# Gate and up: a second set of weight sums, two more raw tiles, accumulators cleared in another order, residual rows kept in DRAM meanwhile

## The chip, the core and the metric

The kernel runs on one core of a Trainium2 chip. Its time is the device time of one execution, in microseconds (us). TensorE (PE) does the matmuls, VectorE (DVE) and ScalarE (ACT) work on tiles, GpSimd (POOL) and SyncE (SP) here mostly issue DMA transfers. Each engine takes its instructions in the order in which they were written to it, and waits where a semaphore is not yet set.

## The reference

One decoder layer over 256 tokens of width 2048, all in float32. The edit lies in the feed-forward part, the third of four:

```python
x = x + mixed @ w_o[i]                        # attention and S5, before it
hf = rms_norm(x, g_ffn_norm[i])
x = x + (jax.nn.silu(hf @ w_gate[i]) * (hf @ w_up[i])) @ w_down[i]   # D_FF = 5632
gate = jax.nn.sigmoid(rms_norm(x, g_ple_norm[i]) @ w_ple_gate[i])    # after it
x = x + gate * (p[i] @ w_ple_proj[i])
```

`x` before the feed-forward part is the residual; in the kernel it is `xs`, four tiles of 128x1024 (512 KB each), which are next needed when the first output block of `w_down` is done.

## The kernel before

**Splitting.** Products keep float32 accuracy by splitting each operand into a high and a low part: ScalarE writes `w_hi` (a rounding copy, L195), VectorE writes `w_lo = w_raw - w_hi` (L196), and each product is three matmuls (hi hi, lo hi, hi lo). The activations `hf` stand in SBUF as `fh` and `fl`.

**Chunks.** Weights come in chunks of 256 rows by 512 columns (512 KB, a tile of 128x2x512), listed in the order of use. `load_to` issues their DMAs on SP into `RAW` = 5 rotating buffers `w_raw`; `split_to` splits them into `PART` = 3 rotating pairs; `take(i)` hands chunk i to PE, after calling for splits and loads ahead of it.

**Gate and up.** 11 blocks of 512 columns. A block has 8 pairs j = 0 to 7, each a gate chunk and an up chunk of the same rows. It adds into four PSUM accumulators: `acc[0]` and `acc[2]` are the gate halves of the two groups of 128 tokens, `acc[1]` and `acc[3]` the up halves. A plain pair is 24 matmuls of 128x512. The pairs in `MIXED` (j = 2, 4, 6; in block 0 only 4, 6) use a Strassen-like scheme: `mix()` builds sums of the weight tiles (`w_sum` on VectorE, then split into `w_last` and two `w_mix`), and seven products replace eight; four more PSUM banks `pp_p` hold shared products, which `shared()` combines into `wsg` and `uc` when a block's last mixed pair is done.

**End of a block.** For each token group t: `wsg += acc[2t]` (VectorE), silu (ScalarE), `uc = acc[2t+1] - uc` (VectorE), `wsg *= uc` (VectorE). Then `gate_task` transposes `wsg` by eight 128x128 matmuls into `pp_g`, and ScalarE copies it to a tile `g`, kept until the down projection. The PSUM banks of the accumulators rotate: the next block writes its `acc[0]`, then from its fourth matmul on `acc[2]`, and from the 13th on `acc[1]` and `acc[3]`, into the banks in the order in which the code releases them.

**Order of the work.** The code is written in the order of the model; a scheduler then orders each engine's instructions by priority and by its own estimate of when inputs are ready. `tc.high_priority(n)` moves instructions ahead; splits and mixing have `W_AHEAD` = 70. `Slots` S is a list of 39 SBUF tiles that the program hands out and takes back (`wait_get`, `wait_n`, `S.put`).

Of the kernel before, what the change touches and what calls it, by code (L numbers as in the profile page):

```python
# [11 lines left out]
F32 = mybir.dt.float32  # L12
F32R = mybir.dt.float32r
I32 = mybir.dt.int32
AF = mybir.ActivationFunctionType
ALU = mybir.AluOpType
# [26 lines left out]
class Slots:  # L43
    def __init__(self, pool, tags):
        self.pool, self.free, self.own = pool, deque(tags), {}
# [36 lines left out]


W_AHEAD = 70

AHEAD = {'s5_params': -50, 'x_stats': 50, 'glu_out': -25, 'gate_task': -25, 'norm_task': -100, 'latent_norms': -50, 'z_task': -200, 'head_norms': -200}

# [54 lines left out]
class Weights:  # L142
# [4 lines left out]
    def __init__(self, tc, pool, sched):  # L147
        self.tc, nc = tc, tc.nc
        self.nc, self.pool, self.sched, self.chunks = nc, pool, sched, []
        self.raw, self.part, self.n_dma, self.n_split = {}, {}, 0, 0  # L150
        self.extra, self.native = {}, set()
        self.mixed, self.kept, self.sums = set(), {}, None

    def block(self, w, k0, nk, c0, n):
        ids = []
# [9 lines left out]
    def load_to(self, i):  # L165
        while self.n_dma <= min(i, len(self.chunks) - 1):
            w, k, c0, n = self.chunks[self.n_dma]
            t = self.pool.tile([128, 2, n], F32, tag="raw", bufs=self.RAW, name="w_raw")
            self.nc.sync.dma_start(
                out=t, in_=w[k * 128:(k + 2) * 128, c0:c0 + n].rearrange("(k p) n -> p k n", p=128)  # L170
            )
            self.raw[self.n_dma] = t
            self.n_dma += 1
            for out, in_ in self.extra.pop(self.n_dma, ()):
                self.nc.sync.dma_start(out=out, in_=in_)

    def split_to(self, i):
        while self.n_split <= min(i, len(self.chunks) - 1):
# [14 lines left out]
            lo = self.pool.tile([128, 2, n], F32R, tag="w_lo", bufs=self.PART, name="w_lo")  # L193
            with self.tc.high_priority(W_AHEAD):
                self.nc.scalar.activation(out=hi, in_=raw, func=AF.Copy)  # L195
# [7 lines left out]
    def mix(self, g, u):  # L203


        V, A, s = self.nc.vector, self.nc.scalar, self.sched
        last, raws, parts = self.sums

        def add(o, a, b):
            V.tensor_tensor(out=o, in0=a, in1=b, op=ALU.add)  # L210

        def part(h, l, r):
            A.activation(out=h, in_=r, func=AF.Copy)  # L213
            V.tensor_tensor(out=l, in0=r, in1=h.bitcast(F32), op=ALU.subtract)  # L214

        with self.tc.high_priority(W_AHEAD):
            add(raws[0][:, 0], g[:, 0], u[:, 0])
            add(raws[0][:, 1], u[:, 0], u[:, 1])
            part(last[:, 0], last[:, 1], u[:, 1])
            add(raws[1][:, 0], raws[0][:, 0], u[:, 1])  # L220
            add(raws[1][:, 1], raws[1][:, 0], g[:, 1])
            for r, (h, l) in zip(raws, parts):
                part(h, l, r)
        s.act += 5 * 512 * 0.83e-3 + 3 * 0.19
        s.dve = max(s.dve + 9 * 512 * 1.05e-3 + 0.42, s.act)
        (h0, l0), (h1, l1) = parts
        return ((last[:, 0], last[:, 1]), (h0[:, 0], l0[:, 0]), (h0[:, 1], l0[:, 1]),
                (h1[:, 0], l1[:, 0]), (h1[:, 1], l1[:, 1])), None, s.dve

    def take(self, i):  # L230
        self.split_to(i + self.PART - 1)
        self.load_to(i + self.PART - 1 + self.RAW)
        hi, lo, t = self.part.pop(i)
        self.sched.pe = max(self.sched.pe, t)
        return hi, lo
# [3 lines left out]
def hybrid_layer_kernel(  # L239
# [6 lines left out]
    nc = tc.nc  # L246
# [7 lines left out]
    dram = ctx.enter_context(tc.tile_pool(name="scratch", bufs=1, space=bass.MemoryType.DRAM))  # L254

    S = Slots(big, [f"s{i}" for i in range(39)])
    PP = Slots(psb, [f"pp{i}" for i in range(4)])
    sched = Sched(tc)
    W = Weights(tc, wts, sched)

    blk = {}
# [28 lines left out]
    def wait_get(shape, name, dtype=F32):  # L290
        n = 0
        while True:
            t = S.try_get(shape, name, dtype)
            if t is not None:
                return t
            sched.step()
            sched.pe += 1.0
            n += 1
            if n > 2000:
                raise RuntimeError(f"no slot for {name}: {S.held()}")  # L300

    def wait_n(n, shape, name, dtype=F32):
        return [wait_get(shape, name, dtype) for _ in range(n)]
# [13 lines left out]
    def stat(name, *dims):  # L317
        return con.tile([128, *dims], F32, name=name)
# [3 lines left out]
    r_a, r_s, r_f, r_p = (stat(n, 2) for n in ("r_a", "r_s", "r_f", "r_p"))  # L322
# [10 lines left out]
    def size(ap):  # L333
        n = 1
        for d in ap.shape[1:]:
            n *= d
        return n
# [4 lines left out]
    def tt(o, a, b, op=ALU.mult):  # L342
        V.tensor_tensor(out=o, in0=a, in1=b, op=op)  # L343
        sched.dve += size(o) * 1.05e-3 + 0.1
# [9 lines left out]
    def act(o, i, f, **k):  # L354
        A.activation(out=o, in_=i, func=f, **k)  # L355
        sched.act += size(o) * 0.83e-3 + 0.19 + 0.09 * sum(n in k for n in ("accum_out",))
# [53 lines left out]
    def accs2():  # L410
        return [psa.tile([128, 512], F32, tag="acc", bufs=4, name="acc") for _ in range(2)]

    def block(ids, lhs, need=None):
        accs = accs2()
        for i, cid in enumerate(ids):
            if need is not None:
                need(W.chunks[cid][1])
            chunk(cid, accs, lhs, i == 0, i == len(ids) - 1)
        return accs
# [23 lines left out]
    NWU = 30  # L443
    X0, B0, NE = 18, 8, 22
    GATE = "y0"


    def s5_params():
# [145 lines left out]
    def s5_tables(rho):  # L594

        while "params" not in sched.flags or rho and GATE not in sched.flags:
            yield None
# [65 lines left out]
    def rot_tables(rho):  # L663

        while "params" not in sched.flags or rho and GATE not in sched.flags:
            yield None
# [452 lines left out]
    def tiles4(hi, lo, k0=0):  # L1119
        def lhs(k, t):  # L1120
            k -= k0
            s = slice(128 * t, 128 * t + 128)
            return hi[k // 4][:, k % 4, s], lo[k // 4][:, k % 4, s]
        return lhs
# [102 lines left out]
    acc = block(blk["zq"], lhs_h, need_h)  # L1227
# [3 lines left out]
    acc = block(blk["zkv"], lhs_h)  # L1231
# [6 lines left out]
    acc = block(blk["u"][0], lhs_h)  # L1238
# [3 lines left out]
    acc = block(blk["u"][1], lhs_h)  # L1242
# [26 lines left out]
    xs = [wait_n(2, [128, 1024], "xs") for _ in range(2)]  # L1269
# [13 lines left out]
    for p, (lo, hi) in enumerate(blk["woa"]):  # L1283
        acc = accs2(), accs2()
# [48 lines left out]
    for b in range(2):  # L1333
        acc = accs2() + accs2()
        ids = blk["glu"][b]
        for i, cid in enumerate(ids):
            w, k, c0, n = W.chunks[cid]
# [21 lines left out]
    fh = wait_n(4, [128, 4, 256], "fh", F32R)  # L1359
    fl = wait_n(4, [128, 4, 256], "fl", F32R)  # L1360
    rows = {j: wait_get([128, 2, 512], "sum", F32R) for j in MIXED}
# [5 lines left out]
    for b in range(4):  # L1367
        acc = block(blk["wos"][b], lhs_s, need_s)
# [6 lines left out]
    lhs_f = tiles4(fh, fl)  # L1375
    wsg = wait_n(2, [128, 2, 512], "wsg")
    uc = wait_get([128, 2, 512], "uc")
    W.sums = (wait_get([128, 2, 512], "w_last", F32R), wait_n(2, [128, 2, 512], "w_sum"),
              [wait_n(2, [128, 2, 512], "w_mix", F32R) for _ in range(2)])
    gr, gh, gl = [], [], []  # L1380

    def gate_task(b):
# [74 lines left out]
    def mixed_block(ids, lhs, rows, a, b, need):  # L1457
        acc = accs2() + accs2()
        pq, left = None, sum(i[2] in W.mixed for i in ids)
        n = left  # L1460
        for i, (j, cg, cu) in enumerate(ids):
            need(j)
            m = cu in W.mixed
            if m and pq is None:
                pq = [wait_pp("p") for _ in range(4)]
            pair(j, cg, cu, acc, pq + [left == n, left == 1] if m else None, lhs, rows, i == 0, i == len(ids) - 1)
            left -= m
            if m and left == 0:
                shared(pq, a, b)
        return acc  # L1470
# [4 lines left out]
    for b in range(11):  # L1475
        ws = wsg[b % 2]
        acc = mixed_block(blk["gu"][b], lhs_f, rows, ws, uc, need_f)
        if b == 0:
            total_rstd(r_f, ss_f)
        for t in range(2):  # L1480
            tt(ws[:, t], ws[:, t], acc[2 * t], ALU.add)
            act(ws[:, t], ws[:, t], AF.Silu, scale=r_f[:, t:t + 1])
            tt(uc[:, t], acc[2 * t + 1], uc[:, t], ALU.subtract)
            tt(ws[:, t], ws[:, t], uc[:, t])
        sched.add(gate_task(b), 0)
    S.put(*fh, *fl, *rows.values(), uc, W.sums[0], *W.sums[1], *W.sums[2][0], *W.sums[2][1])
    lhs_g = tiles4(gh, gl)

    def need_g(k):
# [9 lines left out]
    for b in range(4):  # L1499
        ph.append(wait_get([128, 4, 256], "ph", F32R))  # L1500
        pl.append(wait_get([128, 4, 256], "pl", F32R))
        acc = block(blk["down"][b], lhs_g, need_g)
# [14 lines left out]
    for c in range(4):  # L1517
        acc = block(blk["pp"][c], lambda k, t: (prh[:, k, 128 * t:128 * t + 128],
                                                prl[:, k, 128 * t:128 * t + 128]))
# [9 lines left out]
    for b in range(4):  # L1529
        acc = block(blk["ple"][b], lhs_h2, need_p)  # L1530
        if b == 0:
            total_rstd(r_p, ss_p)
        n = 256 if b == 3 else 512
# [88 lines left out]
```

## Time and profile before

| | |
|---|---|
| time, median of 3 runs | 1145.84 us (1144.41 to 1147.18) |
| profiled execution | 1146.05 us, span 1144.1 us, granted clock 0.998 |
| PE busy | 1117.7 us, 98% of the span |
| VectorE / ScalarE / POOL busy | 861.4 / 648.3 / 19.0 us |
| gate/up stage | 317.77 to 796.63 us in the span, 478.86 us |
| DMA | 216.97 MB, mean 190 GB/s |

A matmul is shown with a modelled duration of 0.39 us, longer than the pace at which matmuls follow each other, so that PE time is best read from start to start. In a timeline a row is: start, duration, engine, line, operation, output<-inputs, shape; the bracket at its end is the idle time of the engine before it and what ended it. A waits row is: waiting instruction <- what it waited for, total us, times, longest. A windows row is: the stretch, its length, the busy time of PE, PE's weight loads, VectorE, ScalarE and POOL with the count of instructions, then granted clock, DMA share and GB/s. `SPq` is SP's DMA queue.

### The profile page before, as it was taken

The numbers are of one execution on the slowest core, as the hardware profiler recorded it, in microseconds if no ns is written. First come the engines' busy times: TensorE is split into PE (matmuls) and PEld (weight loads), VectorE is DVE, ScalarE is ACT, GpSimd is POOL, SyncE is SP. The second block draws the span as 40 slices with busy tenths as digits, with TensorE's granted clock in tenths as the row PEclk, the third lists the DMA queues.
The fourth block names the chain that finished last, engine by engine and source line by source line (L and its number), as shares of the span: only waits on it lengthen the run. The fifth ranks groups of instructions, "written<-read, shape, count | busy, mean of one in ns | idle before, by whom it ended". The sixth has DMA issues, their size and how long they took to land.

```text
span 1144.1 us, 15655 instructions
## 1 busy us (share of the span) xinstructions
PE 1117.7 (98%) x5842; PEld 923.7 (81%) x5842; DVE 861.4 (75%) x1233; ACT 648.3 (57%) x921; POOL 19.0 (2%) x40
## 2 busy tenths in 40 slices
PE   9998999999999999999999999999999999999998
PEld 6877877889887877877877877878888888888886
DVE  7988999658698898888898898899645454546554
ACT  7863994636665555655655655557534344436443
POOL 1000020000000000000000000000000000000000
PEclk9999999999999999999999999999999999999999
DMA  9996471355566656665665665665665655555662
GB/s 336 247 259 191 117 229 33 109 190 179 183 187 200 204 184 185 204 196 180 211 192 178 210 186 178 217 183 184 202 194 186 197 188 191 188 192 187 213 209 91
DMA packets 112188, 216.97 MB, mean 190 GB/s; under 512 B 8032, under 2 KB 12912, under 8 KB 112112
## 3 DMA queue, kind: packets, MB, share of 16 engines
q1 hardware_dynamic: 109808, 211.23, 58.9%
q0 software_dynamic: 2304, 4.74, 1.5%
q8 instruction: 46, 0.75, 0.3%
q14 instruction: 30, 0.25, 0.1%
HBM read 212.66 MB, written 3.28 MB: 189 GB/s over the span
## 4 chain that ended last, share of the span: by engine, by line
PE 78%; DVE 9%; DMA 5%; ACT 4%; issue 2%; POOL 0%; DVEq 0%; SPq 0%; ACTq 0%; POOLq 0%
PE acc L359 67%; PE pp_p L359 5%; DMA w_raw<-in_w_up_dram 4%; DVE w_lo L196 3%; ACT w_hi L195 2%; DMA e<-in_bE_dram 1%; PE pp_g L386 1%; PE pp_at L359 1%; DVE w L750 1%; PE pp_at L1003 1%; PE pp_n L386 1%; PE pp_v L731 1%; DVE w_sum L210 1%; ACT L355 1%; PE pp_y L785 1%
## 5 line engine op out<-in xcount | busy, mean ns | idle before, releaser
L196 DVE TENSOR_TENSOR w_lo<-w_raw,w_hi 128x1024 fp32r<-128x1024 f32 (+2 forms) x350 | 420.8, 1206 | 207.4 <-ACT w_hi L195 206.1
L195 ACT ACTIVATE w_hi<-w_raw 128x1024 fp32r<-128x1024 f32 (+2 forms) x350 | 366.1, 1047 | 350.7 <-PE acc L359 318.9
L359 PE MATMUL acc<-w_hi,fh 128*128 128x512 f32 x480 | 188.7, 396 | 5.9 <-DVE uc L343 5.8
L359 PE MATMUL acc<-w_lo,fh 128*128 128x512 f32 x480 | 188.1, 392 | 0.0
L359 PE MATMUL acc<-w_hi,fl 128*128 128x512 f32 x480 | 187.1, 390 | 0.0
L359 PE MATMUL acc<-w_hi,gh 128*128 128x512 f32 x352 | 137.3, 390 | 0.0
L359 PE MATMUL acc<-w_hi,gl 128*128 128x512 f32 x352 | 137.1, 389 | 0.0
L359 PE MATMUL acc<-w_lo,gh 128*128 128x512 f32 x352 | 137.0, 389 | 0.0
L359 PEld LDWEIGHTS acc<-w_hi,fh 128*128 128x128 f32 x480 | 90.1, 188 | 30.9 <-DVE uc L343 12.4
L359 PEld LDWEIGHTS acc<-w_hi,fl 128*128 128x128 f32 x480 | 90.1, 188 | 18.8
L359 PEld LDWEIGHTS acc<-w_lo,fh 128*128 128x128 f32 x480 | 90.2, 188 | 17.5 <-DVE w_lo L196 0.2
L213 ACT ACTIVATE w_mix<-w_sum 128x1024 fp32r<-128x1024 f32 x64 | 67.9, 1062 | 50.3 <-DVE w_sum L210 38.5
L359 PEld LDWEIGHTS acc<-w_hi,gl 128*128 128x128 f32 x352 | 66.1, 188 | 13.8
L359 PEld LDWEIGHTS acc<-w_lo,gh 128*128 128x128 f32 x352 | 66.1, 188 | 13.6
L359 PEld LDWEIGHTS acc<-w_hi,gh 128*128 128x128 f32 x352 | 66.1, 188 | 13.6 <-DVE uc L343 0.2
L214 DVE TENSOR_TENSOR w_mix<-w_sum,w_mix 128x1024 fp32r<-128x1024 f32 x64 | 76.3, 1218 | 0.6
L359 PE MATMUL pp_p<-w_mix,sum 128*128 128x512 f32 x288 | 70.5, 389 | 0.0
L359 PEld LDWEIGHTS pp_p<-w_mix,sum 128*128 128x128 f32 x288 | 54.1, 188 | 11.2
L210 DVE TENSOR_TENSOR w_sum<-w_raw 128x512 f32<-128x512 f32 x64 | 42.2, 687 | 27.7 <-DMA w_raw<-in_w_up_dram 26.5
L359 PE MATMUL acc<-w_hi,ph 128*128 128x512 f32 x128 | 49.8, 389 | 0.0
L359 PE MATMUL acc<-w_lo,ph 128*128 128x512 f32 x128 | 49.8, 389 | 0.0
L359 PE MATMUL acc<-w_hi,pl 128*128 128x512 f32 x128 | 49.8, 389 | 0.0
(308 smaller groups left out, 1713.0 us busy)
## 6 DMA issues: line engine op xcount, KB each, us to landing
w_raw<-in_w_gate_dram SPq DMA_DIRECT2D x88, 512.0 KB, 4.2
w_raw<-in_w_up_dram SPq DMA_DIRECT2D x88, 512.0 KB, 4.6
w_raw<-in_w_down_dram SPq DMA_DIRECT2D x88, 512.0 KB, 3.7
w_raw<-in_w_o_dram SPq DMA_DIRECT2D x32, 512.0 KB, 3.7
w_raw<-in_w_ple_gate_dram SPq DMA_DIRECT2D x32, 512.0 KB, 4.1
w_raw<-in_w_in_dram SPq DMA_DIRECT2D x24, 512.0 KB, 7.6
w_raw<-in_w_glu_dram SPq DMA_DIRECT2D x8, 512.0 KB, 4.4
w_raw<-in_w_uq_dram SPq DMA_DIRECT2D x8, 384.0 KB, 3.5
```

The source lines that it names most:

```text
L195: self.nc.scalar.activation(out=hi, in_=raw, func=AF.Copy)
L196: self.nc.vector.tensor_tensor(out=lo, in0=raw, in1=hi.bitcast(F32), op=ALU.subtract)
L210: V.tensor_tensor(out=o, in0=a, in1=b, op=ALU.add)
L213: A.activation(out=h, in_=r, func=AF.Copy)
L214: V.tensor_tensor(out=l, in0=r, in1=h.bitcast(F32), op=ALU.subtract)
L355: A.activation(out=o, in_=i, func=f, **k)
L359: T.matmul(out=o, lhsT=a, rhs=b, start=start, stop=stop)
L386: T.transpose(out=o, in_=i, identity=ident if idt is None else idt)
L731: T.matmul(out=pv[p, r * 256 + i4 * 64:r * 256 + i4 * 64 + 64], lhsT=ee[r][p, i * 64:i * 64 + 64], rhs=um[p, i, :], start=True, stop=True, ...
L750: V.tensor_tensor_scan(out=w, data0=dc, data1=w, initial=0.0, op0=ALU.mult, op1=ALU.add)
L785: T.matmul(out=o, lhsT=a[p, i, :], rhs=f[p, i, :], start=False, stop=(r == 1), tile_position=(64 * s, 64 * s))
L1003: T.matmul(out=o, lhsT=a, rhs=b_, start=False, stop=(i == 1), skip_group_check=True)
```

## The change

1. Two more raw tiles `w_more` (from the slots): in the gate/up stage the chunks whose number is 0 or 3 modulo 7 land there, and `take()` calls for loads two chunks further ahead.
2. Two sets of `w_last` and `w_mix` (`NSET` = 2) in turn; `w_sum` stays shared. `take()` now calls for splits so that three plain chunks, and a mixed one behind them, are ready.
3. The end of a block is written in another order (both gate halves, both up halves, both products) and at a high priority, `G_AHEAD` = 100.
4. To make room, the four `xs` tiles are written to DRAM (`x_keep`) and their slots given to the `g` tiles from block 3 on; behind the stage they are read back. Both go by POOL's DMA queue.

```diff
+G_AHEAD = 100
...
-            t = self.pool.tile([128, 2, n], F32, tag="raw", bufs=self.RAW, name="w_raw")
+            if self.more and self.n_dma % 7 in (0, 3) and self.n_dma < self.more_end:
+                self.more.rotate(1)
+                t = self.more[0]
+            else:
+                t = self.pool.tile([128, 2, n], F32, tag="raw", bufs=self.RAW, name="w_raw")
...
-        last, raws, parts = self.sums
+        last, raws, parts = self.sums[0]
+        self.sums.rotate(1)
...
     def take(self, i):
-        self.split_to(i + self.PART - 1)
-        self.load_to(i + self.PART - 1 + self.RAW)
+        n, j = 0, i
+        while n < self.PART and j < len(self.chunks):
+            n += j not in self.mixed
+            j += 1
+        if j in self.mixed:
+            j += 1
+        self.split_to(j - 1)
+        self.load_to(j - 1 + self.RAW + len(self.more))
...
+    NSET = 2
...
-    W.sums = (wait_get([128, 2, 512], "w_last", F32R), wait_n(2, [128, 2, 512], "w_sum"),
-              [wait_n(2, [128, 2, 512], "w_mix", F32R) for _ in range(2)])
+    w_sum = wait_n(2, [128, 2, 512], "w_sum")
+    for _ in range(NSET):
+        W.sums.append((wait_get([128, 2, 512], "w_last", F32R), w_sum,
+                       [wait_n(2, [128, 2, 512], "w_mix", F32R) for _ in range(2)]))
+    W.more_end = blk["down"][0][0]
+    W.more.extend(wait_n(2, [128, 2, 512], "w_more"))
...
-        for t in range(2):
-            tt(ws[:, t], ws[:, t], acc[2 * t], ALU.add)
-            act(ws[:, t], ws[:, t], AF.Silu, scale=r_f[:, t:t + 1])
-            tt(uc[:, t], acc[2 * t + 1], uc[:, t], ALU.subtract)
-            tt(ws[:, t], ws[:, t], uc[:, t])
+        with tc.high_priority(G_AHEAD):
+            for t in range(2):
+                tt(ws[:, t], ws[:, t], acc[2 * t], ALU.add)
+                act(ws[:, t], ws[:, t], AF.Silu, scale=r_f[:, t:t + 1])
+            for t in range(2):
+                tt(uc[:, t], acc[2 * t + 1], uc[:, t], ALU.subtract)
+            for t in range(2):
+                tt(ws[:, t], ws[:, t], uc[:, t])
         sched.add(gate_task(b), 0)
...
+        if b == 2:
+            keep = [dram.tile([128, 1024], F32, name="x_keep") for _ in range(4)]
+            for i in range(4):
+                nc.gpsimd.dma_start(out=keep[i], in_=xs[i // 2][i % 2])
+                S.put(xs[i // 2][i % 2])
...
+    for i in range(4):
+        xs[i // 2][i % 2] = t = wait_get([128, 1024], "xs")
+        nc.gpsimd.dma_start(out=t, in_=keep[i])
```

How it moves instructions, at two places. First VectorE at the boundary from block 2 to block 3; `w_lo` are splits, `w_sum` and `w_last` belong to the next block's first mixed pair, `uc` and `wsg` end the block. Before:

```order
L196 TENSOR_TENSOR w_lo<-w_raw,w_hi 128x1024 x3
L343 TENSOR_TENSOR uc<-wsg,pp_p 128x512
L343 TENSOR_TENSOR wsg<-uc,pp_p 128x512
L343 TENSOR_TENSOR uc<-uc 128x512
L343 TENSOR_TENSOR wsg<-wsg,acc 128x512
L343 TENSOR_TENSOR uc<-wsg,uc 128x512
L210 TENSOR_TENSOR w_sum<-w_raw 128x512 x2
L196 TENSOR_TENSOR w_lo<-w_raw,w_hi 128x1024
L343 TENSOR_TENSOR uc<-acc,uc 128x512
L343 TENSOR_TENSOR wsg<-wsg,acc 128x512
L343 TENSOR_TENSOR wsg<-wsg,uc 128x512
```

The same place in the changed kernel:

```order
L201 TENSOR_TENSOR w_lo<-w_raw,w_hi 128x1024 x4
L216 TENSOR_TENSOR w_sum<-w_more,w_raw 128x512
L355 TENSOR_TENSOR uc<-wsg,pp_p 128x512
L216 TENSOR_TENSOR w_sum<-w_raw 128x512
L355 TENSOR_TENSOR wsg<-uc,pp_p 128x512
L355 TENSOR_TENSOR wsg<-wsg,acc 128x512
L355 TENSOR_TENSOR uc<-uc 128x512
L220 TENSOR_TENSOR w_last<-w_raw,w_last 128x512
L355 TENSOR_TENSOR uc<-wsg,uc 128x512
L201 TENSOR_TENSOR w_lo<-w_more,w_hi 128x1024
L355 TENSOR_TENSOR wsg<-wsg,acc 128x512
L355 TENSOR_TENSOR uc<-acc,uc 128x512 x2
```

The `w_sum` pair has moved ahead of the block's end and now stands in and ahead of the first `uc`; the second accumulator cleared is `acc[2]` (`wsg<-wsg,acc`), no longer `acc[1]` (`uc<-acc,uc`), and the products come last. On PE the eight transposes, which stood as two and six at separate places, stand together behind the next block's first 12 matmuls.

Second, SP's queue where the loads for gate and up begin, at the end of the stage before (`w_o`). Before:

```order
L169 DMA w_raw<-in_w_o_dram 128x2x512 x16
L169 DMA w_raw<-in_w_glu_dram 128x2x512 x8
L169 DMA w_raw<-in_w_o_dram 128x2x512 x16
L169 DMA w_raw<-in_w_gate_dram 128x2x512
L169 DMA w_raw<-in_w_up_dram 128x2x512
```

In the changed kernel:

```order
L174 DMA w_raw<-in_w_glu_dram 128x2x512 x8
L174 DMA w_raw<-in_w_o_dram 128x2x512 x8
L174 DMA w_more<-in_w_gate_dram 128x2x512
L174 DMA w_raw<-in_w_o_dram 128x2x512 x2
L174 DMA w_more<-in_w_up_dram 128x2x512
L174 DMA w_raw<-in_w_o_dram 128x2x512 x6
L174 DMA w_raw<-in_w_gate_dram 128x2x512
L174 DMA w_raw<-in_w_up_dram 128x2x512
```

Two gate/up loads now go out among the last loads of `w_o`; and POOL's queue, which held nothing after the first loads of `xs` but one load near the end, has eight transfers more:

```order
L1285 DMA xs<-in_x_dram 128x1024
L1509 DMA x_keep<-xs 128x1024 x4
L1518 DMA xs<-x_keep 128x1024 x3
L1540 DMA pr_7593<-in_pT_dram 128x512
L1518 DMA xs<-x_keep 128x1024
```

The four writes wait for finished `xs` rows only, which is early in block 0; the reads wait for slots that come free in the last block.

More of the change, by code (lines that the diff above doesn't have):

```diff
@@ L151, in __init__ @@
         self.extra, self.native = {}, set()
-        self.mixed, self.kept, self.sums = set(), {}, None
+        self.mixed, self.kept, self.sums, self.more = set(), {}, deque(), deque()
     def block(self, w, k0, nk, c0, n):
@@ L1479, in hybrid_layer_kernel @@
             total_rstd(r_f, ss_f)
-        for t in range(2):
-            tt(ws[:, t], ws[:, t], acc[2 * t], ALU.add)
-            act(ws[:, t], ws[:, t], AF.Silu, scale=r_f[:, t:t + 1])
-            tt(uc[:, t], acc[2 * t + 1], uc[:, t], ALU.subtract)
-            tt(ws[:, t], ws[:, t], uc[:, t])
-        sched.add(gate_task(b), 0)
-    S.put(*fh, *fl, *rows.values(), uc, W.sums[0], *W.sums[1], *W.sums[2][0], *W.sums[2][1])
+        with tc.high_priority(G_AHEAD):
[6 more added lines that the diff above has]
+                tt(ws[:, t], ws[:, t], uc[:, t])
+        sched.add(gate_task(b), 0)
+        if b == 2:
[3 more added lines that the diff above has]
+                S.put(xs[i // 2][i % 2])
+    more = list(W.more)
+    W.more.clear()
+    S.put(*more, *fh, *fl, *rows.values(), uc, *w_sum)
+    for last, _, parts in W.sums:
+        S.put(last, *parts[0], *parts[1])
+    for i in range(4):
+        xs[i // 2][i % 2] = t = wait_get([128, 1024], "xs")
+        nc.gpsimd.dma_start(out=t, in_=keep[i])
     lhs_g = tiles4(gh, gl)
```

## The prediction

> **What bounds the kernel now.** I read the page first (span, busy shares, the chain), then the waits of the gate/up stage, then the timeline of one block boundary engine by engine, because the change edits only that stage.
>
> ```profile
> span 1144.1 us, 15655 instructions
> PE 1117.7 (98%) x5842; PEld 923.7 (81%) x5842; DVE 861.4 (75%) x1233; ACT 648.3 (57%) x921; POOL 19.0 (2%) x40
> PE 78%; DVE 9%; DMA 5%; ACT 4%; issue 2%; POOL 0%; DVEq 0%; SPq 0%; ACTq 0%; POOLq 0%
> GB/s 336 247 259 191 117 229 33 109 190 179 183 187 200 204 184 185 204 196 180 211 192 178 210 186 178 217 183 184 202 194 186 197 188 191 188 192 187 213 209 91
> ```
>
> TensorE is the bound; what can be won is time in which it does not issue. The windows view of the stage, from its first matmul (317.77) to the first of the down projection (796.63), and its waits:
>
> ```profile
> 317.77:796.63 478.86, 472.18 (x2106) 385.40 (x2105) 419.54 (x507) 281.91 (x324) 0.00 (x0) 1.00 0.63 194
> ```
>
> ```profile
> DVE w_sum L210 <- DMA w_raw<-in_w_up_dram: 26.5, 21, 2.3
> PE acc L359 <- DVE uc L343: 5.8, 9, 1.3
> PE pp_g L386 <- DVE wsg L343: 0.8, 1, 0.8
> ```
>
> PE is idle 478.86 - 472.18 = 6.7 us, and the last two rows name it all: nine waits for a `uc` of VectorE and one for a `wsg`, one at each of the ten boundaries between the eleven blocks. Inside the blocks PE never waits. The granted clock is 1.00. The boundary from block 2 to block 3, on PE:
>
> ```profile
> 442.87 0.39 PE L359 MATMUL acc<-w_hi,fh 128*128 128x512 f32 x1
> ...
> 448.31 0.39 PE L359 MATMUL acc<-w_hi,fh 128*128 128x512 f32 x1
> 448.53 0.39 PE L359 MATMUL acc<-w_lo,fh 128*128 128x512 f32 x1
> 448.76 0.39 PE L359 MATMUL acc<-w_hi,fl 128*128 128x512 f32 x1
> 450.43 0.50 PE L359 MATMUL acc<-w_hi,fh 128*128 128x512 f32 x1 [1.28 <-DVE uc L343]
> 450.77 0.39 PE L359 MATMUL acc<-w_lo,fh 128*128 128x512 f32 x1
> ```
>
> From 442.87 to 448.76 are 26 matmuls, 0.2267 us each: the pace. 448.31 is the first matmul of block 3; call it B. The fourth, which writes the second accumulator, should start at B+0.68 and starts 1.44 us late (450.43 - 448.76 - 0.23); the one after it is another 0.11 late (0.34 instead of 0.23). What VectorE did meanwhile:
>
> ```profile
> 442.39 0.69 DVE L343 TENSOR_TENSOR uc<-wsg,pp_p 128x512 f32<-128x512 f32 x1 [0.33 <-PE pp_p L359]
> 443.11 0.69 DVE L343 TENSOR_TENSOR wsg<-uc,pp_p 128x512 f32<-128x512 f32 x1
> 443.90 0.69 DVE L343 TENSOR_TENSOR uc<-uc 128x512 f32<-128x512 f32 x1
> 444.51 0.68 DVE L343 TENSOR_TENSOR wsg<-wsg,acc 128x512 f32<-128x512 f32 x1
> 445.11 0.69 DVE L343 TENSOR_TENSOR uc<-wsg,uc 128x512 f32<-128x512 f32 x1
> 447.35 1.29 DVE L210 TENSOR_TENSOR w_sum<-w_raw 128x512 f32<-128x512 f32 x2 [1.56 <-DMA w_raw<-in_w_up_dram]
> 448.56 1.22 DVE L196 TENSOR_TENSOR w_lo<-w_raw,w_hi 128x1024 fp32r<-128x1024 f32 x1
> 449.70 0.68 DVE L343 TENSOR_TENSOR uc<-acc,uc 128x512 f32<-128x512 f32 x1
> 450.30 0.67 DVE L343 TENSOR_TENSOR wsg<-wsg,acc 128x512 f32<-128x512 f32 x1
> ```
>
> VectorE works in order. It stands at the `w_sum` of the next block's first mixed pair until that pair's up load lands, and only then clears `acc[1]` (449.70 to 450.38), whose bank the new second accumulator takes. The load was issued late, because with five raw buffers it waits for a split made at the boundary itself. The queue of SP, and the ScalarE split that stands a block's last gate chunk ahead:
>
> ```profile
> 437.98 0.37 SPq L169 DMA_DIRECT2D w_raw<-in_w_up_dram  x1
> 440.65 0.37 SPq L169 DMA_DIRECT2D w_raw<-in_w_gate_dram  x1
> 442.09 0.37 SPq L169 DMA_DIRECT2D w_raw<-in_w_up_dram  x1
> 449.80 0.37 SPq L169 DMA_DIRECT2D w_raw<-in_w_gate_dram  x1
> ```
>
> ```profile
> 435.63 1.06 ACT L195 ACTIVATE w_hi<-w_raw 128x1024 fp32r<-128x1024 f32 x1 [1.66 <-PE acc L359]
> 445.86 1.04 ACT L195 ACTIVATE w_hi<-w_raw 128x1024 fp32r<-128x1024 f32 x1
> ```
>
> **How much there is to win.** The stage runs 2,016 matmuls of 128x512 and 88 transposes of 128x128: 2016 x 0.2267 + 88 x 0.095 = 465.4 us, against 478.9. Of the 13.5 us of excess, start-to-start differences like those above put 12.8 at the ten boundaries (1.77, 1.23, 1.94, 1.08, 0.85, 1.00, 1.24, 1.18, 0.93, 1.59), counting the gap, the slower matmul behind it, and about 0.09 behind each of the two groups of transposes:
>
> ```profile
> 365.89 0.44 PE L386 MATMUL pp_g<-ident,wsg 128*128 128x128 f32 x2 [0.78 <-DVE wsg L343]
> 369.71 0.82 PE L386 MATMUL pp_g<-ident,wsg 128*128 128x128 f32 x6
> ```
>
> So 12.8 us (1.1%) is the ceiling of the gain.
>
> **The change, part by part.**
>
> *Two more raw tiles.* A chunk now takes the place of the one seven, not five, ahead of it. The up load of the next block's first mixed pair then waits for the split of the block's last gate chunk: ScalarE at 435.63, VectorE's half done by 437.9. It is issued when the load at 437.98 was: B-10.33, where now it goes at 442.09 = B-6.22. Its landing is the disputed number. These are the whole stage's up loads (min/median/max), and the single gate load of 449.80, which has no load within 7 us ahead of it:
>
> ```profile
> DMA to landing us min/median/max: 4.3/4.6/5.2
> DMA to landing us min/median/max: 3.5/3.5/3.5
> ```
>
> The load at 442.09 had a gate load 1.44 us ahead and was usable at 447.35, L = 5.26 after issue. In the new order the nearest load ahead left a whole split earlier, so I take it as nearly alone: L = 3.6 to 3.9, with 3.5 and 5.3 as ends. `w_sum` can then start at B-6.7 to B-6.4; it is 0.5 us ahead of what follows it and VectorE stops waiting there.
>
> *Order of the epilogue and its priority.* On VectorE the new order from there is w_sum, uc, w_sum, wsg, wsg+acc[0], uc, w_last, uc, w_lo, wsg+acc[2]: back to back at 0.60 each (444.51 to 445.11), 0.72 where the next needs the one before (442.39 to 443.11), 1.14 for w_lo (448.56 to 449.70), 0.68 for the last: 6.74, with a second dependence 6.85. Three floors for its end: from the load, B-10.33 + L + 6.85, which is B+0.1 to B+0.4; from the first `uc`, which waits for PE as it does now (442.39 = B-5.92), B+0.2; from the w_lo, whose ScalarE half is at 445.86 now (it ends at 446.90, B-1.41, and VectorE follows at once), +1.14 +0.68 = B+0.41. PE wants it at B+0.68, and the second bank released is now that of `acc[2]`, which PE finishes before `acc[1]`. So there is no gap, with 0.27 us to spare; a load at L = 4.16 or more costs what it is later, one for one. `acc[1]` and `acc[3]` are cleared 0.6 and 1.2 us behind; PE wants those banks at B+2.72.
>
> *Later products.* Both `wsg` products now come last, at 0.60 each behind the two `uc`: B+2.9 to B+3.0. All eight transposes stand together behind the first 12 matmuls, where the second needs the product of the second half at about B+2.9: up to 0.12 us of wait, and 0.09 behind one group in place of two. I allow 0.14 more for boundaries where ScalarE comes later than at this one and the 0.27 us does not cover it (a gap brings the 0.11 above with it). Residue: 0.35 a boundary, 3.5 for ten. Queued behind the clearing are the splits of the second pair; VectorE ends the first near B+4.6 and PE comes to it behind 24 matmuls, at B+5.4, so the priority costs nothing while this 0.8 lasts.
>
> *Two sets of w_last and w_mix, and the new look-ahead.* Mixing can start while PE reads the other set. Inside the blocks PE waits for no mix, so nothing is gained; the instructions are the same in number. In block 0 the mixing goes ahead of the last four `fl` splits, 0.41 us each (1.66 for four), wanted only by the last pair: 0, bounded by 1.7 us.
>
> *Residual rows in DRAM.* Eight transfers of 512 KB on POOL, which is 2% busy. Its issues and landings so far, and the first use of the rows in the down stage:
>
> ```profile
> L1272 POOL DMA_DIRECT2D xs<-in_x_dram x4: 530/560/587, 143.0 to 165.4; - x4
> DMA to landing us min/median/max: 4.2/6.9/10.5
> L351 DVE SCALAR_TENSOR_TENSOR xs<-acc,r_f,xs x8: 740/743/746, 857.2 to 1040.1; 128x512 f32<-128x512 f32 x8
> ```
>
> The writes need only finished rows, so they go out in block 0, near 318; the reads go out in the last block, the last near 797, sixty us ahead of 857.2. POOL's issues (8 x 0.56) hold nobody. What they can do is delay weight loads beside them, at two places, between 0 and 6 us each (10.5 less 4.4).
>
> *Sum.* 12.8 - 3.5 = 9.3 us off the profiled execution, which took 1146.05 (span 1144.1 and 1.95 around it) and stands 0.2 above the median of 1145.84: 1146.05 - 9.3 - 0.2 = 1136.5 us.
>
> **The rivals.** Faster or slower means by over 0.2% (2.3 us), about what a measurement of this kernel can tell from no change.
>
> 1. *The load lands as late as the up loads do now.* For: all up loads took 4.3 or more. Against: a gate load ran just ahead of those that VectorE waited for. With L = 4.5 the gap is 0.34, the transposes wait 0.25, and a boundary costs 0.8: gain 4.8, 1141 us. From L = 4.76 the gain is under 2.3 and reads as no change; at 4.9 it is 1145.
>
> 2. *Seven loads in flight share the engines so that L passes 5.2.* Then each boundary costs 1.5 and more, and the kernel is slower by over 2.3 us; at L = 5.6, ten times 1.9 less 12.8: plus 6, 1152. For: the 5.26 above. Against: the rate stays 194 GB/s, and loads are issued as buffers come free, one by one.
>
> 3. *The keep traffic starves the weights (the other side).* Place: block 0, from 318, and the first down loads. It decides where it eats more than 9.3 + 2.3 us: two times 5.8, just inside the bound of 6 each. That gives up to 1149. For: POOL's loads of the same size took up to 10.5 beside SP's. Against: block 0 moves some 190 to 200 GB/s (187 and 200 in the page's slices from 315 to 372 us) and the first slice 336, so the spare rate carries 2.1 MB in 15 us, and raw tiles are read seven chunks ahead. [...]
>
> 4. *The wait stays in the transposes alone* is in the residue: 0.12 to 0.25.
>
> **How the numbers follow.** Floors hold, L up to 4.16 (1133.5 to 1139): 0.52. Rival 1 with a gain over 2.3 (1139 to 1143.5): 0.22; rival 1 as no change (1143.5 to 1148): 0.14. Rival 2: 0.05. Rival 3: 0.07. Faster 0.52 + 0.22 = 0.74, same 0.14, slower 0.12. The range 1133.5 to 1145 leaves out rivals 2 and 3, some of the no-change case, and a little below: under 0.2. The low end is a residue of nothing.
>
> **What would show it.** Right: `w_sum <- DMA` at the boundaries nearly gone from the waits; `PE acc <- DVE uc` 5.8 us down to under 1; PE's idle time in the stage from 6.7 to under 2; the stage near 469.5 us; up loads ahead of a boundary issued at B-10.3 and landing in under 4. Wrong: VectorE still waiting for the up load with `wsg` the new releaser (rival 1 or 2, told apart by L); PE waiting for w_lo or w_mix near 320 to 345 or at 797 (rival 3). A prediction that fails by more than 5 us fails on L.

## The result, and the profile after

| | before | changed |
|---|---|---|
| median | 1145.28 us (1144.41 to 1147.18, 4 runs) | 1139.13 us (1137.72 to 1140.31, 4 runs) |
| ratio, 95% interval | | 0.9942 [0.9926, 0.9958] |
| profiled execution | 1146.05 us | 1137.72 us |

The change makes the kernel 0.4 to 0.7% faster. 1136.5 was forecast, in a range of 1133.5 to 1145: the sign and the range hold, the gain (9.3 forecast, 6.2 between the medians) was over-estimated by half. The profiled execution is the fastest of the four, so its difference of 8.3 us flatters the change. The page of the changed kernel, and its gate/up stage from first matmul to the first of the down projection (columns as before: stretch, length, PE, PE's weight loads, VectorE, ScalarE, POOL, clock, DMA share, GB/s):

```profile
span 1136.0 us, 15630 instructions
PE 1114.4 (98%) x5842; PEld 925.8 (81%) x5842; DVE 857.8 (76%) x1233; ACT 645.6 (57%) x921; POOL 23.3 (2%) x48
316.76:787.33 470.57, 468.82 (x2106) 386.88 (x2105) 416.33 (x507) 281.92 (x326) 4.14 (x8) 1.00 0.65 203
```

The stage fell from 478.86 to 470.57 us, 8.3 less; PE's idle time in it from 6.7 to 1.75. Ahead of the stage the changed kernel is 1.0 us earlier (316.76 for 317.77) with nearly the same work: over the profiles of all kernels here that point lies anywhere from 316.4 to 320.8, so 1.0 us is within that scatter. Behind the stage it is 1.2 us longer (1136.0 - 787.33 = 348.67 for 347.47). What the edit did is thus 8.3 - 1.2 = 7.1 us in this pair of profiles. The waits of PE and of VectorE's first weight sum from 317 to 796 us, which reaches 9 us into the down projection:

```profile
DVE w_sum L216 <- DMA w_raw<-in_w_up_dram: 7.3, 8, 3.1
DVE w_sum L216 <- DMA w_more<-in_w_up_dram: 3.4, 3, 1.3
PE acc L371 <- DVE uc L355: 0.9, 1, 0.9
PE acc L371 <- DVE wsg L355: 0.8, 2, 0.4
PE acc L371 <- DVE w_lo L201: 0.6, 2, 0.4
PE pp_g L398 <- DVE wsg L355: 0.4, 1, 0.4
```

Where there were 26.5 us of `w_sum` waiting and 5.8 of PE waiting for `uc`, there are 10.7 and 0.9. Most of the `w_sum` waiting lies inside the blocks, and of that only one wait of 3.1 us, in block 0, reaches PE in the changed kernel; at the ten boundaries it was 9.4 us and is 2.3. The 0.9 lies 4 us behind the stage, at the start of down; the two waits for `w_lo` are in block 0. The boundary from block 2 to block 3 again, SP's queue, VectorE and PE:

```profile
433.38 3.84 SPq L174 DMA_DIRECT2D w_raw<-in_w_up_dram  x2
```

```profile
441.15 0.69 DVE L216 TENSOR_TENSOR w_sum<-w_more,w_raw 128x512 f32<-128x512 f32 x1 [0.22 <-DMA w_raw<-in_w_up_dram]
441.77 0.68 DVE L355 TENSOR_TENSOR uc<-wsg,pp_p 128x512 f32<-128x512 f32 x1
...
445.99 1.23 DVE L201 TENSOR_TENSOR w_lo<-w_more,w_hi 128x1024 fp32r<-128x1024 f32 x1
447.13 0.68 DVE L355 TENSOR_TENSOR wsg<-wsg,acc 128x512 f32<-128x512 f32 x1
447.73 1.28 DVE L355 TENSOR_TENSOR uc<-acc,uc 128x512 f32<-128x512 f32 x2
```

```profile
447.19 0.39 PE L371 MATMUL acc<-w_hi,fh 128*128 128x512 f32 x1
...
447.64 0.39 PE L371 MATMUL acc<-w_hi,fl 128*128 128x512 f32 x1
447.86 0.49 PE L371 MATMUL acc<-w_hi,fh 128*128 128x512 f32 x1
```

Here B = 447.19. The second of the two up loads went out at 436.85 (433.38 + 3.84 - 0.37), B-10.34, and was usable at 441.15: L = 4.30. `acc[2]` is cleared at 447.81 and PE starts its matmul at 447.86, on time.

### The profile page after: what moved, and what is told of

The parts are those of the page before. It is cut to its first block, busy times and chain, and to the rows that moved or that the text cites. A ratio compares the mean times of both kernels' runs of the same rounds, so it can differ in the third digit from the quotient of the medians.

```text
span 1136.0 us, 15630 instructions
## 1 busy us (share of the span) xinstructions
PE 1114.4 (98%) x5842; PEld 925.8 (81%) x5842; DVE 857.8 (76%) x1233; ACT 645.6 (57%) x921; POOL 23.3 (2%) x48
## 4 chain that ended last, share of the span: by engine, by line
PE 78%; DVE 11%; DMA 4%; issue 3%; ACT 3%; SPq 0%; DVEq 0%; ACTq 0%
PE acc L371 66%; PE pp_p L371 6%; DVE w_lo L201 3%; DMA w_raw<-in_w_up_dram 1%; DMA e<-in_bE_dram 1%; DMA w_raw<-in_w_in_dram 1%; DVE w_sum L216 1%; PE pp_at L371 1%; ACT w_hi L200 1%; DVE w_mix L220 1%; PE pp_g L398 1%; DVE w L763 1%; PE pp_at L1016 1%; DVE gl L355 1%; DVE uc L355 1%
## 5 line engine op out<-in xcount | busy, mean ns | idle before, releaser
L201 DVE TENSOR_TENSOR w_lo<-w_raw,w_hi 128x1024 fp32r<-128x1024 f32 (+2 forms) x309 | 372.2, 1205 | 213.2 <-ACT w_hi L200 212.2
L200 ACT ACTIVATE w_hi<-w_raw 128x1024 fp32r<-128x1024 f32 (+2 forms) x309 | 322.8, 1045 | 345.7 <-PE acc L371 266.5
L371 PEld LDWEIGHTS acc<-w_lo,fh 128*128 128x128 f32 x480 | 90.2, 188 | 19.4 <-DVE w_lo L201 1.4
L200 ACT ACTIVATE w_hi<-w_more 128x1024 fp32r<-128x1024 f32 x41 | 43.3, 1055 | 36.4 <-issue 21.0
L201 DVE TENSOR_TENSOR w_lo<-w_more,w_hi 128x1024 fp32r<-128x1024 f32 x41 | 50.1, 1221 | 11.4 <-ACT w_hi L200 11.1
```

The lines of the kernel that those rows point to most:

```text
L201: self.nc.vector.tensor_tensor(out=lo, in0=raw, in1=hi.bitcast(F32), op=ALU.subtract)
L371: T.matmul(out=o, lhsT=a, rhs=b, start=start, stop=stop)
```

## The experiments

All times are medians against runs of the kernel before on the same chip; "stage" and "behind" are read from each profile as above (before: 478.86 and 347.47).

| run | what of the change | us | ratio [95%] | stage | behind |
|---|---|---|---|---|---|
| e1 | block's end only, order and priority | 1140.58 | 0.9936 [0.9919, 0.9953] | 472.44 | 347.45 |
| e5 | order only | 1144.63 | 0.9984 [0.9970, 0.9997] | 476.93 | 347.48 |
| e6 | priority only | 1141.42 | 0.9955 [0.9937, 0.9973] | 472.47 | 347.45 |
| e9 | raw tiles and `xs` in DRAM | 1139.97 | 0.9949 [0.9931, 0.9967] | 472.91 | 347.44 |
| e10 | e9 and the block's end, without the priority in the last block | 1140.44 | 0.9952 [0.9935, 0.9969] | 471.73 | 347.58 |
| e7 | all but the block's end | 1194.22 | 1.0415 [1.0397, 1.0434] | 526.01 | 347.84 |
| e12 | the changed kernel again | 1140.62 | 0.9953 [0.9937, 0.9968] | 470.87 | 348.73 |
| e11 | changed, no priority in the last block | 1140.68 | 0.9951 [0.9932, 0.9970] | 472.07 | 348.57 |
| e3 | changed, `xs` writes meant to be later | 1140.64 | 0.9944 [0.9929, 0.9959] | 470.28 | 349.18 |
| e4 | changed, no `xs` in DRAM | 1139.82 | 0.9941 [0.9924, 0.9958] | 468.69 | 350.46 |
| e2 | raw tiles (faulty, see there) | 1150.86 | 1.0039 [1.0023, 1.0055] | 481.72 | 347.88 |
| e8 | raw tiles, `xs` in DRAM (faulty) | 1154.90 | 1.0069 [1.0047, 1.0091] | 486.03 | 348.09 |

**e1: the block's end alone.** Against the kernel before, shortened, with comments added here:

```diff
-        for t in range(2):                # the old order, as in the kernel before
+        with tc.high_priority(G_AHEAD):   # the new order, as in the changed kernel
...
# RAW = 5, one set of sums, no w_more, no x_keep, take() as before
```

> Only the order and priority of the block's end are changed; five raw buffers, one set of weight sums, xs stays in SBUF. Theory A (the earlier load is what removes the wait): the up load still goes out at B-6.2 and VectorE still waits for it, so the gaps on PE stay above 0.4 us a boundary and the gain is at most 3 us (1142 or more). Theory B (the order is enough: VectorE needs only one w_sum of 0.6 and then clears acc[2], at about B+0.3 for a load that is usable at B-1.0): PE's gaps fall under 0.2 us a boundary and the gain is 6 to 9 us (1136 to 1139). I lean to B at two to one.

The whole gain in the measured time, by theory B. Its waits and the same boundary (B = 449.16):

```profile
DVE w_sum L216 <- DMA w_raw<-in_w_up_dram: 26.3, 20, 3.2
PE pp_g L392 <- DVE wsg L349: 2.2, 7, 0.7
```

```profile
445.96 0.69 DVE L349 TENSOR_TENSOR uc<-wsg,uc 128x512 f32<-128x512 f32 x1
447.25 0.69 DVE L216 TENSOR_TENSOR w_sum<-w_raw 128x512 f32<-128x512 f32 x1 [0.60 <-DMA w_raw<-in_w_up_dram]
447.86 0.68 DVE L349 TENSOR_TENSOR wsg<-wsg,acc 128x512 f32<-128x512 f32 x1
448.45 1.22 DVE L201 TENSOR_TENSOR w_lo<-w_raw,w_hi 128x1024 fp32r<-128x1024 f32 x1
449.59 1.28 DVE L349 TENSOR_TENSOR uc<-acc,uc 128x512 f32<-128x512 f32 x2
```

VectorE waits for the up load as long as before (26.3 us), and at the accumulators it costs PE nothing: one `w_sum` of 0.6 us, not two and a split, stands between the landing and `acc[2]`, cleared at 448.54 = B-0.62, where PE wants it at B+0.68. The wait for the load was not the loss by itself; what stood behind it ahead of the clearing was. What PE still loses stands at the transposes: 2.2 us in seven waits for a product `wsg`.

**e5 and e6: order or priority.** e5 keeps the new written order and drops the `with`; e6 keeps the `with` around the old order; nothing else of the change.

> Only the written order of the block's end (both gate halves, both up halves, both products), without the priority; nothing else of the change. Theory P (what counts is that all four clearings stand ahead of mixing and splits on VectorE, which the priority does): w_sum, w_last and two splits still stand between acc[2] and acc[3], whose clearing ends near B+5 while PE wants it near B+3.4: the gap moves to a later matmul, about 1.5 us a boundary, and the kernel is within 3 us of the kernel before or slower (1143 to 1150). Theory O (the written order is enough, since acc[2] now comes second): 1139 to 1141.

> Only the high priority, with the old written order; nothing else of the change. Theory P: VectorE gets the same order at nine of ten boundaries as with both, so the gain is the same, 1139 to 1141.5. Theory O: no gain, 1144 or more.

Theory P in both. e6 is e1 within the noise, 472.47 to 472.44 in the stage: with the priority the scheduler puts VectorE's instructions in the same order whatever was written (of 506 in the stage, two differ in place). In e5 the gap moved to another bank:

```profile
PE acc L365 <- DVE uc L349: 6.7, 10, 1.0
452.11 0.68 DVE L349 TENSOR_TENSOR uc<-acc,uc 128x512 f32<-128x512 f32 x1
452.85 0.50 PE L365 MATMUL acc<-w_hi,fh 128*128 128x512 f32 x1 [0.78 <-DVE uc L349]
```

The last `uc` (`acc[3]`), behind a `w_sum`, `w_last` and two splits, ends at 452.79 and PE goes on at 452.85. Ten gaps of 0.6 to 1.1 us remain; about 0.2 us a boundary is won (478.86 to 476.93).

**e2 and e8: raw tiles, a faulty build.** Two more raw tiles, `NSET` = 1, old end of block, `take()` as before; e8 also keeps `xs` in DRAM.

> Only the two more raw tiles; old order and priority of the block's end, one set of sums, xs in SBUF. Theory A: the up load goes out near B-10.3, is usable near B-6.5, VectorE no longer waits for it, acc[1] is cleared by B+0.5 at the boundaries where nothing else stands ahead of it; gain 5 to 8 us (1137 to 1140). Theory B: w_sum, w_last and the splits that the scheduler now puts ahead of uc<-acc delay the clearing as much as the load did; gain under 3 us.

> Two more raw tiles and xs in DRAM, one set of sums, old end of block. In the run with the raw tiles alone (where late slots also moved work) PE waited for w_mix inside the blocks. Theory S (one set of sums is what limits an earlier mix: the mix must wait for PE's last use, and PE then waits for the mix): waits pp_p <- w_mix of 2 us or more in sum, boundary gaps small, total 1141 to 1148. Rival (those waits came from the slots): no such waits, and the gain of the early load shows, 1138 to 1141.

Both are slower, and say nothing on the early load. With `take()` as before, the last load ahead is written to a `w_more` tile whose gate chunk is still to be mixed; the mix then reads a later chunk's data and waits for that load (25.9 us of `w_sum` waiting for `w_more` in e2). (So both compute other sums than the kernel.) e8's theory S, that one set of sums limits an earlier mix, is not settled by this; e9 answers it.

**e9: the raw tiles, mended.** As e8, with

```diff
-        self.load_to(i + self.PART - 1 + self.RAW + len(self.more))
+        self.load_to(i + self.PART - 1 + self.RAW + max(0, len(self.more) - 1))
```

> Two more raw tiles and xs in DRAM alone, with the look-ahead one load shorter (in the two earlier runs of this kind the last load ahead went into a tile whose gate chunk a mix had yet to read, so that mixes waited for loads of later data; they say nothing on the early load). One set of sums, old end of block without priority. Theory A' (the early load is enough by itself: w_sum runs ahead, acc[1] is cleared near B+0.45): boundary gaps under 0.3 us, 1138 to 1141, the same gain as the priority alone. Theory P only (without the priority no gain): 1144 or more.

Theory A'. With the old end of block and no priority, the early load alone gives 0.9949. From 317 to 796 us:

```profile
DVE w_sum L216 <- DMA w_raw<-in_w_up_dram: 5.2, 3, 4.2
DVE w_sum L216 <- DMA w_more<-in_w_up_dram: 1.2, 1, 1.2
PE acc L365 <- DVE uc L349: 0.7, 2, 0.5
```

`w_sum` waits for loads 6.4 us in place of 26.5, 4.2 of them once in block 0, and no wait of PE for `w_mix` shows, with one set of sums. One thing is not as in the changed kernel: the reads of `x_keep`, which wait for free slots, go out in block 0 too (321.28 to 340.96; in the changed kernel 757.20 to 781.51), right behind the writes. e8 and e10 have this too.

**e10: both.** e9 with the block's end in the new order, and at the priority in all blocks but the last.

> Early load and priority together, but one set of sums, xs written behind block 2, and no priority in the last block. If the two remove the same wait, they do not add: 1137 to 1140, stage 469 to 472, and no 0.9 us gap at the start of down. If the second set of sums matters, waits of PE for w_mix return and it is 1141 or more.

In the measured time the two do not add: 0.9952 beside 0.9936 to 0.9955 for either. For the most part they remove the same wait. The profiles show the rest when the stage is cut at the first matmul of block 2 (us, from each profile):

| | before | e6 | e1 | e9 | e10 | changed | e12 |
|---|---|---|---|---|---|---|---|
| blocks 0 and 1 | 87.08 | 86.61 | 87.05 | 89.29 | 88.71 | 87.97 | 87.65 |
| blocks 2 to 10 | 391.78 | 385.87 | 385.39 | 383.62 | 383.02 | 382.60 | 383.22 |

In blocks 2 to 10 the early load is worth about 2 us more than the priority, and both together a little more again. The kernels with the early load pay this back in blocks 0 and 1, where the DRAM copy runs (see e4).

**e7: all but the block's end.** The changed kernel with the old order and no priority.

> The changed kernel with the old order and no priority at the block's end: two more raw tiles, two sets of sums and xs in DRAM stay. Theory Q (whatever stands ahead of the clearings on VectorE sets the boundary): loads land early and two sets let the whole mixing of the next pair, two w_mix and the splits go ahead of the first clearing, which ends near B+4.4 in place of B+0: 3 to 5 us a boundary lost, 1170 to 1195. Theory A of the prediction (the early load is what removes the wait): a gain of 4 us or more, under 1142.

Theory Q, at the upper end: 48 us slower. The two sets, with the look-ahead of their `take()`, let mixing start early, and on VectorE it then stands ahead of the clearings. PE's waits from 317 to 846 us, and the boundary from block 1 to block 2:

```profile
PE acc L371 <- DVE wsg L355: 20.2, 10, 2.1
PE pp_p L371 <- DVE w_mix L220: 15.2, 10, 2.4
```

```profile
411.43 0.68 DVE L216 TENSOR_TENSOR w_sum<-w_sum,w_raw 128x512 f32<-128x512 f32 x1
412.03 1.22 DVE L220 TENSOR_TENSOR w_mix<-w_sum,w_mix 128x1024 fp32r<-128x1024 f32 x1
413.17 1.22 DVE L201 TENSOR_TENSOR w_lo<-w_raw,w_hi 128x1024 fp32r<-128x1024 f32 x1
414.30 1.22 DVE L220 TENSOR_TENSOR w_mix<-w_sum,w_mix 128x1024 fp32r<-128x1024 f32 x1
415.44 0.68 DVE L355 TENSOR_TENSOR wsg<-wsg,acc 128x512 f32<-128x512 f32 x1
```

```profile
411.66 0.39 PE L371 MATMUL pp_p<-w_mix,sum 128*128 128x512 f32 x1
413.30 0.73 PE L371 MATMUL pp_p<-w_mix,sum 128*128 128x512 f32 x2 [1.25 <-DVE w_mix L220]
416.17 0.80 PE L371 MATMUL acc<-w_hi,fh 128*128 128x512 f32 x1 [2.13 <-DVE wsg L355]
416.76 0.63 PE L371 MATMUL acc<-w_lo,fh 128*128 128x512 f32 x1
```

On VectorE only the first clearing is shown; it ends at 416.12, and PE starts the next block's first pair there. PE's order has changed too: three matmuls of that block's first mixed pair (`pp_p<-w_mix`, 411.66 and 413.30) stand ahead of its first pair, and PE waits for their `w_mix` as well; the clearing comes later and decides. So the block's end as the change writes it is what makes the two sets bearable, and nothing that they bring is seen in any time.

**e3 and e4: the DRAM copy.** e3 puts a copy of one column of block 2's `wsg` ahead of the four writes on POOL; e4 leaves the DRAM copy out.

> The changed kernel, but POOL waits for the end of block 2 before it writes xs to DRAM (a one-column copy of wsg ahead of the writes). Theory K (the writes at 316 to 325 us delay the weight loads of block 0): the two waits of PE for w_lo near 332 and 338 us (1.1 us with what follows) and part of the loss at the first boundary (1.4 us) go, about 2 us better than the changed kernel, and w_up issued at 322 lands in under 5 us in place of 6.4; a loss of up to 1 us may show behind block 2. Rival (mixing went ahead of the splits in block 0 and costs this by itself): block 0 as in the changed kernel, within 0.4 us.

> The changed kernel without the DRAM copy of xs: g and gh/gl tiles get their slots later. Theory K: block 0 as in the run with the late writes, and no gap of 0.9 us at the start of the down projection, since fewer gl splits stand ahead of the last uc on VectorE: 2 to 3.5 us better than the changed kernel (1135.5 to 1137). Rival (the room is needed): gh/gl tiles come late, PE waits for them at the start of down, 1 to 10 us worse than the changed kernel.

e3 tested nothing: POOL's queue shows the last three of the four writes at 320.73 to 322.73 (the first goes out ahead of the stage, at 298.04) and the copy behind them at 410.29, since the scheduler ordered the writes ahead of it. It stands as another run of the changed kernel. In e10 and e11 the same copy was to hold the writes back, and did not. In e4 the slots run out: the transposes of the last four blocks come behind the stage, when `wsg` has been overwritten, so only its first blocks compare. There the load of block 0's first mixed pair (the first of SP's two; changed kernel, then e4):

```profile
322.07 3.36 SPq L174 DMA_DIRECT2D w_raw<-in_w_up_dram  x2
328.63 1.29 DVE L216 TENSOR_TENSOR w_sum<-w_raw 128x512 f32<-128x512 f32 x2 [3.06 <-DMA w_raw<-in_w_up_dram]
...
331.81 0.50 PE L371 MATMUL acc<-w_lo,fh 128*128 128x512 f32 x1 [0.17 <-DVE w_lo L201]
337.95 0.50 PE L371 MATMUL acc<-w_lo,fh 128*128 128x512 f32 x1 [0.38 <-DVE w_lo L201]
```

```profile
322.77 3.36 SPq L174 DMA_DIRECT2D w_raw<-in_w_up_dram  x2
327.49 1.29 DVE L216 TENSOR_TENSOR w_sum<-w_raw 128x512 f32<-128x512 f32 x2 [1.24 <-DMA w_raw<-in_w_up_dram]
```

6.56 us from issue to use beside the writes, 4.72 without them. The same load took 6.4 to 6.6 us in the five profiles that have the writes alone in block 0, and 7.8 to 8.1 in e8, e9 and e10, where the reads run there too. PE waits behind this in all eight and in none of the six without the copy: block 0 lasts 44.1 to 44.2 us, 45.1 to 45.4 with the reads, and 43.1 without the copy. Theory K holds for block 0. The boundary behind it goes the same way: the up load for block 1 went out at B-9.40 in the changed kernel (B-9.47 to B-9.59 in e3 and e9 to e12) and at B-10.20 in e4, the one profile with this look-ahead and no copy. Blocks 0 and 1 together last 85.51 us in e4 and 87.1 to 88.0 in the changed kernel, e3, e11 and e12, so by this one profile the copy costs 1.6 to 2.5 us there.

**e11 and e12: the start of down.** e11 uses the priority in blocks 0 to 9 only.

> The changed kernel with the xs writes behind block 2 and no priority in the last block. Expected: what lies behind the stage falls back from 348.7 to 347.5 us, the stage stays near 470; 1 to 2 us better than the changed kernel. Rival (the 0.9 us gap is the gl splits' and has nothing to do with the priority): as the changed kernel.

> The changed kernel once more, beside these three on the same chip: 0.993 to 0.996 of the kernel before.

e11's rival holds: 348.57 behind the stage, as in e12 (348.73). The profiles with an extra 1 us there (changed, e3, e11, e12: 348.6 to 349.2) have the two sets with their look-ahead; with raw tiles and DRAM copy but one set (e9, and e10 with the priority) it is 347.4 to 347.6. e7, with two sets and the old end, has 347.84. The two groups differ in a second thing: in the first the reads of `x_keep` end just ahead of down, in e9 and e10 they ran in block 0. Which of the two brings the extra, and why e7 pays less, was not tried.

No run beats the changed kernel beyond the intervals. e1 equals it with none of the buffers and no DRAM traffic.

## Why the prediction was right, and where it was off

- **What bounds the stage** held: clearing late at the ten boundaries, behind a `w_sum`. Removing it by any of three ways (e6, e9, both) takes the stage to 470.3 to 472.9 us.
- **The ceiling** of 12.8 was read half a microsecond low. Its fifth and ninth entries, 0.85 and 0.93, are short: at the ninth boundary the gap ahead of the fourth matmul (0.86) and the slower one behind it (0.11) are more than 0.93 by themselves. Counted alike for all ten (from the fourth matmul ahead of a boundary to the 46th of the new block, less 0.2267 a matmul and 0.095 a transpose), these two are 1.06 and 1.37 and the sum is 13.36.
- **L** was forecast at 3.6 to 3.9. At seven of ten boundaries `w_sum` started 3.99 to 4.01 us after the issue without waiting for the load, so it had landed by then; the landings in the trace are 3.55 to 3.81 at six of them and 3.99 at one. At the three others it waited, to L = 4.54, 4.30 and 4.83. The rule "from 4.16 on, one for one" held roughly: 4.30 is just on time above, and 4.83 brings a gap of 0.53 at the second accumulator. One boundary of ten as late as 4.8 was not in the residue. The issue at B-10.33 came at B-10.32 to B-10.34 at nine boundaries; at the first it came at B-9.40, and there the gap is 0.60 with L = 4.54, in another order on VectorE.
- **Residue.** Forecast 3.5 us for ten boundaries and none elsewhere. Measured by the count above: eight boundaries at 0.14 to 0.35 each, the one from block 4 to 5 0.89, the first 1.51 (gaps of 0.60 and 0.54 and what follows them), 3.92 in all; and 1.14 in block 0, which the sum had at 0 with a bound of 1.7, and for another reason than the order of its splits. So the ten boundaries came out near the forecast, and the step that was mis-sized is the first block, where the DRAM writes run, priced as free. The sum with these sizes, 13.36 - 3.92 - 1.14 = 8.30, is what the stage fell by.
- **The last boundary** was not in the sum: 1.2 us behind the stage, a `uc` behind a `gl` split at the start of down. It leaves 7.1 us between the two profiles. The medians say 6.2; the profiled execution of the changed kernel was its fastest.
- **The DRAM copy** as rival 3 was right in its first place and in its sign, and far from its bound: one load 1.8 us later, not 6, and 1.6 to 2.5 us in the first two blocks. From issue to use that load took 4.72 us in e4 without the copy, 6.4 to 6.6 beside the writes alone, and 7.8 to 8.1 with the reads as well; how POOL's and SP's queues share the DMA engines was not shown.
- **The reason given was half wrong.** "A prediction that fails by more than 5 us fails on L" made the early load the thing on which the gain hangs. e1 and e6 show the gain with the load as late as ever, because the priority takes the second `w_sum` and the splits from between the load and the clearing. The early load is enough (e9) and not needed for most of the gain. That two parts of a change each do the whole was not among the rivals.

## What to carry to other kernels

On VectorE, which here worked in order, the wait for the load cost little by itself: e1 has 26.3 us of it, for 26.5 before, and its stage fell from 478.86 to 472.44 us. What cost was the work between that wait and the instruction that others wait for (two `w_sum` and a split before, one `w_sum` of 0.6 us in e1); so move that instruction ahead before buying buffers to shorten the wait. When a change has several parts that aim at one stall, price each alone: here either of two gives the whole gain in time, they do not add, and a third (the second set of sums with its look-ahead) makes the kernel 48 us slower than before without the new end of block. Room made by moving tiles to DRAM was paid here in the loads that ran beside the copies: 1.6 to 2.5 us by one profile, about what the early load brought beyond the priority.

## What was not expected of the hardware

In e7 the granted clock of the span is 0.981, where the other profiles have 0.995 to 0.998. The windows at the boundary shown (stretch, length, PE, PE's weight loads, VectorE, ScalarE, POOL, clock, DMA share, GB/s):

```profile
411.00:414.00 3.00, 1.75 (x7) 0.85 (x5) 3.00 (x4) 2.00 (x2) 0.00 (x0) 1.00 0.78 208
414.00:416.00 2.00, 0.04 (x1) 0.00 (x0) 2.00 (x3) 0.00 (x0) 0.00 (x0) 0.94 0.76 213
416.00:418.00 2.00, 1.83 (x4) 1.50 (x5) 1.65 (x4) 1.61 (x3) 0.00 (x0) 0.50 0.65 237
418.00:420.00 2.00, 2.00 (x8) 1.60 (x7) 2.00 (x4) 0.24 (x1) 0.00 (x0) 0.70 0.02 7
420.00:422.00 2.00, 2.00 (x13) 1.64 (x12) 1.00 (x3) 1.06 (x1) 0.00 (x0) 1.00 0.04 8
```

Three matmuls started in the 4.5 us from 411.66 to 416.17; then the granted clock was 0.50 from 416 to 418. If it was at one half or at full in the rows beside that one too (0.94 and 0.70), it was at one half for about 3.4 us (0.2 + 2 + 1.2), an estimate. By the counts in the rows some eleven matmuls (4 and 8, one of them cut by the edge at 418) started in the 3.83 us from 416.17 to 420, which at 0.2267 us each would be 2.5: by this estimate another 1.3 us at this boundary on top of 3.8 of gaps, so that the gaps were dearer here than their sum.

What lowered the clock the profiles do not settle. In e7 the longest idle time at this boundary was 2.13 us, with two matmuls ahead of it and 1.25 before those. The longest gap in the stage of the kernel before, 1.44 us (1.28 of it idle) with busy PE on both sides, left the clock at 1.00. Ahead of the stage, PE's idle time of 2.90 us up to 90.22 in the kernel before was followed by 0.58 (90.2 to 92) and 0.52 (92 to 94), and that of 2.12 us up to 184.29 in the changed kernel by 0.50 (184.29 to 187); but the same gap in the kernel before, 2.11 us up to 186.32, and one of 2.45 us up to 89.75 in the changed kernel left it at 1.00. So the length of one gap does not tell it here, and whether the two gaps close together did it in e7 was not tried.
